# Six of the eight weight tiles of a first column block, split in advance into high and low halves

## The chip, the cores and the metric

The kernel runs on one core of one Trainium2 chip. The metric is the device time of one launch in microseconds. Engines are named as in the profile: PE is TensorE (PEld its weight loads), DVE is VectorE, ACT is ScalarE, POOL is GpSimd and SP is SyncE, which here only issues DMAs. POOL issues DMAs too.

## The reference, cut to what matters

Two blocks run one after the other on a sequence of 512 tokens with 1024 features, all in float32.

```python
def first_block(x, ...):
    x = x + 0.5 * swiglu(rmsnorm(x, ffn1_norm), ...)      # first gated layer
    ... two attentions ...
    x = x + 0.5 * swiglu(rmsnorm(x, ffn2_norm), ...)      # second gated layer: 1024 -> 2816 -> 1024
    x = rmsnorm(x, final_norm)
    return x

def token_mix(h, w_in, ...):                              # the mixer of the second block
    p = h @ w_in                                          # 1024 -> 2848
    ... convolution, recurrent scan ...
    return jnp.concatenate([u, y], axis=-1) @ w_out

def channel_mix(h, w_up, ...):
    z = causal_dwconv(h @ w_up, ffn_dw_w, ffn_dw_b)
    ...
```

`swiglu` is `(silu(h @ w_gate) * (h @ w_up)) @ w_down`. The change concerns the first 768 columns of the mixer's `w_in`: what is multiplied by them stays as it is.

## The kernel before, in words

**The three-part product.** Activations lie with features on the 128 partitions and tokens along the free axis. Every float32 operand is split into two parts, a rounded high half and the rest as a low half, and a product is three matmuls: high by high, high weight by low activation, low weight by high activation (`mm3`, L386). So every weight tile needs a split. `split_weights` (L375) does it at the time of use: SP issues the read into a `raw` tile, ACT copies it into the high half (L378), and DVE subtracts to get the low half (L379). There are two `raw` buffers, so a read waits until DVE is done with the read before the last one.

**Halves made in advance.** Some weights are split earlier and kept in DRAM. `make_halves` (L353) gives a list of pieces. A piece reads half the columns of one K tile (128 rows) into the one buffer `pre0` (POOL's queue, L363), DVE rounds it into `pre1` (the CAST of L365) and subtracts into `pre2` (L366), and POOL issues two writes to DRAM (L368). Each of the three buffers exists once. So the read of the next piece can start only after the subtraction of this one, and on POOL's queue it stands behind this one's two writes. Before the change the list has 32 pieces: 16 of 512 columns (`w_out2`, shown in some rows as `w_out`) and 16 of 384 columns (`up2k`). `halves_at` (L347) later loads both halves as they are, with two reads on SP's queue.

**Where the pieces run.** `swiglu` (L567) of the second gated layer takes two lists of side work, the modulation's (18 entries) and the pieces. Its first loop makes 22 pairs of gate and up column blocks and takes one entry of each list per pair. Its second loop, the down phase, makes output column blocks 0 to 6 (K = 2816, so 22 K tiles in weight chunks of 8, 8 and 6), and spreads over them what is left of the lists:

```python
n = -(-len(side) // (last - m))
weave(self.dense_steps(lambda: ps, down[m], hs, split=4), [(1.3, f) for f in side[:n]])
```

Block 7 follows in two halves of 256 tokens (`dense_halves`, L448). In the down phase only two weight slots exist, so the split of a chunk starts when PE has left the chunk before the last. At the end of a block `done` (L616) adds the result to `x` (L619, L620), sums squares (L512) and has POOL write `x` to DRAM (L624).

**Order.** The tile framework puts the instructions of each engine into one fixed order when the program is built, by its own estimates; a piece's two DVE operations stand at places in DVE's order that were chosen then. At run time each engine takes its instructions in that order.

**The mixer's first column blocks.** `first` (L1053) multiplies K tile by K tile into six column blocks at once (`group_halves`, L465): for each K tile the six products for tokens 0 to 255, then a second round for tokens 256 to 511. The split weights of all eight K tiles are kept for the second round, the first two in the ordinary weight slots and the others in buffers `kb`, `ra` and `vt` that the mixer uses later for something else (`room`, L1039). Those buffers lie in memory that the gated layer used before. While it runs, `enter(1, k)` (L659) prepares the second half of the tokens.

Of the kernel before, what the change touches and what calls it, by code (L numbers as in the profile page):

```python
# [11 lines left out]
F32 = mybir.dt.float32  # L12
# [7 lines left out]
P = 128  # L20
T = 512
D = 1024
KD = D // P
# [15 lines left out]
W_IN2 = [n for p in PH for n in p.split() if n[0] != "t" and n != "d1"]  # L39
# [216 lines left out]
class Net:  # L256
# [96 lines left out]
    def make_halves(self):  # L353


        nc, A = self.nc, self.A
        parts = ("w_out2", D), ("up2k", 768)
        self.made = {n: self.pd.tile([2, KD, P, w], F32, tag=n, name=n) for n, w in parts}

        def piece(name, k, c):  # L360
            n = c.stop - c.start
            raw, hi, lo = (self.pt.tile([P, T], dt, tag=f"pre{j}", name=f"pre{self._n()}") for j, dt in enumerate((F32, F32R, F32R)))
            nc.gpsimd.dma_start(raw[:, :n], A[name][k][:, c])  # L363
            with self.tc.issue_after(self.anchor):
                nc.vector.tensor_copy(hi[:, :n], raw[:, :n])  # L365
                nc.vector.tensor_sub(lo[:, :n], raw[:, :n], hi[:, :n].bitcast(F32))  # L366
            for half, t in enumerate((hi, lo)):
                nc.gpsimd.dma_start(self.made[name][half, k][:, c], t[:, :n].bitcast(F32))  # L368

        return [  # L370
            lambda name=name, k=k, c=c: piece(name, k, c)
            for name, w in parts for k in range(KD) for c in (slice(0, w // 2), slice(w // 2, w))
        ]

    def split_weights(self, raw, hi, lo, src, n):  # L375
# [608 lines left out]
    def mixer(self, acc1, acc2, stop):  # L984
        nc, A = self.nc, self.A
        nfg, dY, xs = self.nfg, self.dY, self.xin
# [15 lines left out]
        with self.phase("mix", False) as pa:  # L1002
# [49 lines left out]

            def first():  # L1053
                side = {2 + n: [lambda k=k: self.enter(1, k)] for n, k in enumerate((None, *range(KD)))}
                self.group_halves(lambda k, *a: self.weights_at(A["w_in2k"][k], *a), 6, xs, room, side, done=lambda m, ps: done(W_IN2[m])(ps), W=2)

            def residual():

# [4 lines left out]
            def shifted(j, out):  # L1063


                def f(ps):
                    n = ps.shape[0]
                    mu = self.v("mu", j)[:n]
                    nc.scalar.activation(out, ps, AF.Copy, scale=mu1[:n, j : j + 1])
                    nc.vector.scalar_tensor_tensor(  # L1070
                        out[:, 1:], ps[:, : T - 1], mu, out[:, 1:], op0=ALU.mult, op1=ALU.add
                    )

                return f
# [7 lines left out]
            def done(name):  # L1082
                if name == "w":
                    return shifted(0, wa)
                return {"k": k_done, "r": r_done, "v": v_done, "u": u_done, "g": ug_done, "d": gd_done}[name[0]](int(name[1]))
# [178 lines left out]
            def gate(f):  # L1264
# [5 lines left out]
                if f == 3:  # L1270
                    gt.extend((xt_(6), xt_(7), keep([P, T], "gd0"), keep([P, T], "gd1")))
                    for n, t in enumerate(gt):
                        nc.scalar.copy(t, st["gate", n])

            first()
            residual()
            ra = [keep([P, 2, T], f"ra{f}") for f in range(4)]
# [422 lines left out]
```

## Time and profile before

| What | us |
|---|---|
| median of 3 runs (lowest to highest) | 1691.19 (1685.33 to 1691.64) |
| profiled execution | 1682.04 |
| its span | 1680.3 |
| PE busy | 1647.0 (98%) |
| DVE busy | 1035.1 (62%) |
| ACT busy | 704.7 (42%) |
| POOL busy | 106.3 (6%) |

The profiled execution is one run; its span is what the views of the trace divide up, from 0 to 1680.3 us, and 1.7 us lie around it. Times in the rows are counted from the start of the span. A row of the timeline has the start and the length in us, the engine, the line, the operation, the output and the inputs, how many instructions were merged, and in brackets how long the engine stood idle before it and what ended that idle time.

### The profile page before, as it was taken

Reading aid. Unit: us, or ns where it says so; the run is one execution under the profiler, and the core shown is the slowest. Engines: PE = TensorE matmul, PEld = TensorE weight load, DVE = VectorE, ACT = ScalarE, POOL = GpSimd, SP = SyncE. Lnnn points to the kernel's source line nnn. Section 1 sums busy time; section 2 is a strip of 40 time slices with the busy share of each in tenths; the row PEclk is TensorE's granted clock in tenths of the full one; section 3 lists DMA queues with packets and bytes.
Section 4 is the critical chain, followed back from the end, with each engine's and each line's share of the span. In section 5 each row is a group of like instructions: output and inputs, shape, how many; then the busy total and the mean of one; then the engine's idle time right before and its main releaser. Section 6 shows DMA issues by size and latency. Waiting matters only on the chain.

```text
span 1680.3 us, 22030 instructions
## 1 busy us (share of the span) xinstructions
PE 1647.0 (98%) x8596; PEld 1334.7 (79%) x8596; DVE 1035.1 (62%) x1754; ACT 704.7 (42%) x1151; POOL 106.3 (6%) x200
## 2 busy tenths in 40 slices
PE   9999999999999999999999999999989999999997
PEld 6888888876776788888888887786869988888886
DVE  4554545546889565666445468998856675665224
ACT  5432232237669552232223254733346454444222
POOL 0000000000000002221122110000010000000000
PEclk9999999999999999999999999997989999999998
DMA  5344445534121226665455442232244023323332
GB/s 205 117 147 144 139 128 194 175 101 135 51 63 33 74 90 223 216 211 198 150 178 182 140 124 69 76 93 88 70 154 168 27 88 101 99 90 97 100 95 85
DMA packets 73081, 206.54 MB, mean 123 GB/s; under 512 B 18857, under 2 KB 21161, under 8 KB 72976
## 3 DMA queue, kind: packets, MB, share of 16 engines
q1 hardware_dynamic: 54320, 146.30, 26.9%
q0 software_dynamic: 16784, 56.73, 10.2%
q10 hardware_dynamic: 1872, 2.10, 0.4%
q8 instruction: 67, 1.10, 0.3%
q14 instruction: 38, 0.31, 0.1%
HBM read 183.87 MB, written 21.23 MB: 122 GB/s over the span
## 4 chain that ended last, share of the span: by engine, by line
PE 88%; DVE 6%; issue 2%; ACT 2%; DMA 2%; POOL 0%; ACTq 0%; DVEq 0%; POOLq 0%
PE ps L321 86%; PE ps L899 1%; DMA raw<-in_ffn_k 1%; DVE acc L512 1%; DVE Ts L1196 1%; DVE Tm L1193 0%; DVE wlo L379 0%; DMA Ts<-dY 0%; DMA raw<-in_w_in2k 0%; DVE x L1551 0%; DVE f L1645 0%; PE ps L1356 0%; DVE x L1646 0%; DVE x L1552 0%; ACT sq L511 0%
## 5 line engine op out<-in xcount | busy, mean ns | idle before, releaser
L378 ACT CAST whi<-raw 128x1024 fp32r<-128x1024 f32 (+1 forms) x240 | 245.3, 1022 | 625.7 <-PE ps L321 584.1
L379 DVE TENSOR_TENSOR wlo<-raw,whi 128x1024 fp32r<-128x1024 f32 (+1 forms) x240 | 284.5, 1186 | 238.0 <-ACT whi L378 232.9
L321 PE MATMUL ps<-xh,whi 128*128 128x512 f32 (+1 forms) x1008 | 400.0, 398 | 1.1 <-ACT xh L542 1.0
L321 PE MATMUL ps<-xh,wlo 128*128 128x512 f32 (+1 forms) x1008 | 390.9, 389 | 1.7 <-DVE wlo L379 1.6
L321 PE MATMUL ps<-xl,whi 128*128 128x512 f32 (+1 forms) x1008 | 391.0, 388 | 0.8 <-DVE xl L543 0.8
L321 PEld LDWEIGHTS ps<-xh,whi 128*128 128x128 f32 x1008 | 189.2, 188 | 51.5 <-issue 5.8
L321 PEld LDWEIGHTS ps<-xl,whi 128*128 128x128 f32 x1008 | 189.3, 188 | 44.5 <-issue 5.3
L321 PEld LDWEIGHTS ps<-xh,wlo 128*128 128x128 f32 x1008 | 188.9, 188 | 42.6 <-DVE wlo L379 2.8
L321 PE MATMUL ps<-hh,whi 128*128 128x512 f32 (+1 forms) x560 | 210.5, 376 | 0.0
L321 PE MATMUL ps<-hh,wlo 128*128 128x512 f32 (+1 forms) x560 | 209.8, 375 | 0.0
L321 PE MATMUL ps<-hl,whi 128*128 128x512 f32 (+1 forms) x560 | 209.8, 375 | 0.0
L321 PE MATMUL ps<-oh,whi 128*128 128x512 f32 (+1 forms) x360 | 134.5, 374 | 0.0
L321 PE MATMUL ps<-ol,whi 128*128 128x512 f32 (+1 forms) x360 | 134.1, 372 | 0.0
L321 PE MATMUL ps<-oh,wlo 128*128 128x512 f32 (+1 forms) x360 | 134.0, 372 | 0.0
L321 PEld LDWEIGHTS ps<-hh,whi 128*128 128x128 f32 x560 | 105.4, 188 | 19.7 <-issue 0.8
L321 PEld LDWEIGHTS ps<-hl,whi 128*128 128x128 f32 x560 | 105.4, 188 | 18.9
L321 PEld LDWEIGHTS ps<-hh,wlo 128*128 128x128 f32 x560 | 105.4, 188 | 18.9
L583 DVE TENSOR_TENSOR s<-s,ps 128x512 f32<-128x512 f32 x44 | 30.1, 687 | 133.0 <-PE ps L321 133.0
L321 PEld LDWEIGHTS ps<-oh,whi 128*128 128x128 f32 x360 | 67.7, 188 | 12.2 <-PE ps L321 0.2
L321 PEld LDWEIGHTS ps<-ol,whi 128*128 128x128 f32 x360 | 67.8, 188 | 12.1 <-issue 0.2
L321 PEld LDWEIGHTS ps<-oh,wlo 128*128 128x128 f32 x360 | 67.8, 188 | 11.8
L581 DVE TENSOR_TENSOR s<-ps,r 128x512 f32<-128x512 f32 x44 | 30.2, 691 | 56.0 <-PE ps L321 55.9
(446 smaller groups left out, 2237.2 us busy)
## 6 DMA issues: line engine op xcount, KB each, us to landing
raw<-in_ffn_gu SPq DMA_DIRECT2D x82, 512.0 KB, 4.2
ada<-in_ada_w POOLq DMA_DIRECT2D x48, 512.0 KB, 4.3
raw<-in_up SPq DMA_DIRECT2D x38, 512.0 KB, 3.5
raw<-in_ffn_d SPq DMA_DIRECT2D x32, 512.0 KB, 3.9
raw<-in_w_in SPq DMA_DIRECT2D x27, 512.0 KB, 3.5
w_out<-pre POOLq DMA_DIRECT2D x32, 256.0 KB, 4.6
raw<-in_down SPq DMA_DIRECT2D x16, 512.0 KB, 3.5
raw<-in_ffn_d SPq DMA_DIRECT2D x16, 384.0 KB, 3.1
```

What stands on the lines that cost most here:

```text
L321: self.nc.tensor.matmul(*a, **k)
L378: nc.scalar.copy(hi[:, :n], raw[:, :n])
L379: nc.vector.tensor_sub(lo[:, :n], raw[:, :n], hi[:, :n].bitcast(F32))
L512: nc.vector.tensor_add(acc, acc, s)
L581: nc.vector.tensor_mul(s, pg, r)
L583: self.anchor = nc.vector.tensor_mul(s, s, pu).ins
L899: nc.tensor.transpose(ps[:, i * P : (i + 1) * P], es[u, i][:, j * P : (j + 1) * P], self.c("ident"))
L1196: ins = nc.vector.tensor_add(t[:, i + 1 :, :c], t[:, i + 1 :, :c], o)
```

## The change

`make_halves` gets a third list of pieces, put ahead of the other two: K tiles 2 to 7 of the mixer's first 768 columns, 12 pieces of 384 columns. `first` then loads those six K tiles with `halves_at`, two reads each; K tiles 0 and 1 are split at the time of use as before.

```diff
@@ make_halves
-        parts = ("w_out2", D), ("up2k", 768)
-        self.made = {n: self.pd.tile([2, KD, P, w], F32, tag=n, name=n) for n, w in parts}
+        parts = ("w_in2k", 768, range(2, KD)), ("w_out2", D, range(KD)), ("up2k", 768, range(KD))
+        self.made = {n: self.pd.tile([2, KD, P, w], F32, tag=n, name=n) for n, w, _ in parts}
...
-            for name, w in parts for k in range(KD) for c in (slice(0, w // 2), slice(w // 2, w))
+            for name, w, ks in parts for k in ks for c in (slice(0, w // 2), slice(w // 2, w))
@@ mixer, first
-                self.group_halves(lambda k, *a: self.weights_at(A["w_in2k"][k], *a), 6, xs, room, side, done=lambda m, ps: done(W_IN2[m])(ps), W=2)
+                load = lambda k, *a: self.weights_at(A["w_in2k"][k], *a) if k < 2 else self.halves_at("w_in2k", k, *a)
+                self.group_halves(load, 6, xs, room, side, done=lambda m, ps: done(W_IN2[m])(ps), W=2)
```

The list of pieces grows from 32 to 44. The gate and up loop still takes 22 of them, so 22 are left for the down phase where there were 10.

DVE's order around one block of the down phase, block 5, before. `s` and `x` are the end of block 4, `wlo` the low halves of the weight chunks, `pre` the pieces, `acc` the sums of squares.

```order
L619 TENSOR_TENSOR s_7264<-ps_7171,r_4880 128x512
L620 TENSOR_TENSOR x_75<-x_75,s_7264 128x512
L379 TENSOR_TENSOR wlo_7307<-raw_7305,whi_7306 128x1024
L512 TENSOR_TENSOR acc_4875<-acc_4875,sq_7267 128x512
L365 CAST pre_7324<-pre_7323 128x384
L366 TENSOR_TENSOR pre_7325<-pre_7323,pre_7324 128x384
L512 TENSOR_TENSOR acc_4872<-acc_4872,sq_7270 128x512
L379 TENSOR_TENSOR wlo_7345<-raw_7343,whi_7344 128x768
L379 TENSOR_TENSOR wlo_7380<-raw_7378,whi_7379 128x1024
L619 TENSOR_TENSOR s_7367<-ps_7274,r_4880 128x512
```

And the same place of the changed kernel.

```order
L620 TENSOR_TENSOR x_75<-x_75,s_7329 128x512
L379 TENSOR_TENSOR wlo_7380<-raw_7378,whi_7379 128x1024
L512 TENSOR_TENSOR acc_4876<-acc_4876,sq_7332 128x512
L365 CAST pre_7316<-pre_7315 128x384
L366 TENSOR_TENSOR pre_7317<-pre_7315,pre_7316 128x384
L512 TENSOR_TENSOR acc_4872<-acc_4872,sq_7335 128x512
L379 TENSOR_TENSOR wlo_7418<-raw_7416,whi_7417 128x768
L365 CAST pre_7359<-pre_7358 128x384
L366 TENSOR_TENSOR pre_7360<-pre_7358,pre_7359 128x384
L365 CAST pre_7397<-pre_7396 128x384
L366 TENSOR_TENSOR pre_7398<-pre_7396,pre_7397 128x384
L379 TENSOR_TENSOR wlo_7461<-raw_7459,whi_7460 128x1024
```

One piece has become three, and two of them stand back to back ahead of the low half of the next chunk.

SP's queue at the start of the mixer, before: the reads for K tiles 1 to 5 of `first`, each into one of the two `raw` buffers.

```order
L377 DMA raw_7761<-in_w_in2k 128x768
L377 DMA raw_7785<-in_w_in2k 128x768
L377 DMA raw_7818<-in_w_in2k 128x768
L377 DMA raw_7845<-in_w_in2k 128x768
L377 DMA raw_7872<-in_w_in2k 128x768
```

And now, from K tile 1 on; `in_w_in` are the weights of the column blocks that follow `first`, `w_in2k` without the `in` the halves kept in DRAM.

```order
L377 DMA raw_7858<-in_w_in2k 128x768
L377 DMA raw_8218<-in_w_in 128x1024
L377 DMA raw_8260<-in_w_in 128x1024
L350 DMA kb_1101_7880<-w_in2k 128x768
L350 DMA kb_1102_7881<-w_in2k 128x768
L350 DMA kb_1105_7911<-w_in2k 128x768
L350 DMA kb_1106_7912<-w_in2k 128x768
L350 DMA ra_1107_7936<-w_in2k 128x768
L350 DMA ra_1108_7937<-w_in2k 128x768
L350 DMA ra_1109_7961<-w_in2k 128x768
L350 DMA ra_1110_7962<-w_in2k 128x768
L350 DMA vt_7986<-w_in2k 128x768 x4
```

Six reads became twelve, and two reads for later blocks now stand ahead of all twelve; each of the two needs a `raw` buffer, so the second waits until DVE has split K tile 1.

## Rows read from the trace of the kernel before

**Rows 1.** The page: busy time, share of the span and count by engine

```profile
PE 1647.0 (98%) x8596; PEld 1334.7 (79%) x8596; DVE 1035.1 (62%) x1754; ACT 704.7 (42%) x1151; POOL 106.3 (6%) x200
```

**Rows 2.** Busy time by stretch: length, engines, granted clock, DMA share, GB/s

```profile
862.00:963.00 101.00, 101.00 (x447) 83.65 (x446) 45.08 (x62) 27.61 (x32) 19.89 (x37) 1.00 0.54 173
984.00:1004.50 20.50, 16.81 (x121) 14.95 (x122) 14.76 (x29) 11.29 (x21) 3.56 (x11) 1.00 0.54 161
```

**Rows 3.** Timeline of DVE in the down phase, pieces and what stands between

```profile
865.59 0.36 DVE L365 CAST pre<-pre 128x384 fp32r<-128x384 f32 x1
...
871.01 0.36 DVE L365 CAST pre<-pre 128x384 fp32r<-128x384 f32 x1 [4.47 <-DMA pre<-in_up2k]
871.40 0.56 DVE L366 TENSOR_TENSOR pre<-pre,pre 128x384 fp32r<-128x384 f32 x1
...
876.62 0.36 DVE L365 CAST pre<-pre 128x384 fp32r<-128x384 f32 x1 [1.73 <-DMA pre<-in_up2k]
876.90 1.22 DVE L379 TENSOR_TENSOR wlo<-raw,whi 128x1024 fp32r<-128x1024 f32 x1
...
884.82 0.36 DVE L365 CAST pre<-pre 128x384 fp32r<-128x384 f32 x1 [4.26 <-DMA pre<-in_up2k]
...
890.45 0.40 DVE L365 CAST pre<-pre 128x384 fp32r<-128x384 f32 x1 [0.60 <-DMA pre<-in_up2k]
...
897.15 0.36 DVE L365 CAST pre<-pre 128x384 fp32r<-128x384 f32 x1 [1.68 <-DMA pre<-in_up2k]
```

**Rows 4.** Timeline of POOL in the same stretch: the issues of the pieces' reads

```profile
867.36 0.54 POOL L363 DMA_DIRECT2D pre<-in_up2k  x1
...
872.78 0.54 POOL L363 DMA_DIRECT2D pre<-in_up2k  x1
...
879.41 0.54 POOL L363 DMA_DIRECT2D pre<-in_up2k  x1
...
886.60 0.54 POOL L363 DMA_DIRECT2D pre<-in_up2k  x1
...
893.87 0.54 POOL L363 DMA_DIRECT2D pre<-in_up2k  x1
```

**Rows 5.** The tile `in_up2k`: the reads of the 384-column pieces

```profile
L363 POOL DMA_DIRECT2D pre<-in_up2k x16: 541/541/543, 797.1 to 938.2; - x16
...
DMA to landing us min/median/max: 2.8/3.2/5.3
```

**Rows 6.** Timeline of DVE at the ends of blocks 5 and 6

```profile
948.27 0.69 DVE L619 TENSOR_TENSOR s<-ps,r 128x512 f32<-128x512 f32 x1 [2.00 <-PE ps L321]
...
963.23 0.69 DVE L619 TENSOR_TENSOR s<-ps,r 128x512 f32<-128x512 f32 x1 [2.00 <-PE ps L321]
...
964.57 1.22 DVE L379 TENSOR_TENSOR wlo<-raw,whi 128x1024 fp32r<-128x1024 f32 x1
```

**Rows 7.** DMA issues: the 512-column pieces' reads, KB each, median us to landing

```profile
pre<-in_w_out POOLq DMA_DIRECT2D x16, 256.0 KB, 5.0
```

**Rows 8.** Timeline of PE in the mixer's first round: its waits, and K tile 7

```profile
986.80 0.38 PE L321 MATMUL ps<-xh,kb 128*128 128x256 f32 x1 [0.53 <-ACT kb L378]
...
991.25 0.38 PE L321 MATMUL ps<-xh,kb 128*128 128x256 f32 x1 [1.21 <-ACT kb L378]
...
992.25 0.50 PE L321 MATMUL ps<-xh,kb 128*128 128x256 f32 x2 [0.49 <-DVE kb L379]
...
1001.93 0.68 PE L321 MATMUL ps<-xh,vt 128*128 128x256 f32 x1
```

**Rows 9.** Timeline of SP: the issue of the read for K tile 3

```profile
985.30 0.33 SPq L377 DMA_DIRECT2D raw<-in_w_in2k  x1
```

**Rows 10.** Busy time by stretch, while the halves of `up2k` are loaded

```profile
1287.00:1289.00 2.00, 2.00 (x19) 2.00 (x18) 2.00 (x7) 0.84 (x2) 0.00 (x0) 1.00 0.82 318
```

**Rows 11.** Timeline of PE after a wait in the scan

```profile
1228.91 0.38 PE L321 MATMUL ps<-oh,kb 128*128 128x256 f32 x1 [1.76 <-ACT oh L383]
```

**Rows 12.** Busy time by stretch, some us behind that wait

```profile
1232.00:1234.00 2.00, 2.00 (x12) 2.00 (x10) 0.00 (x0) 0.00 (x0) 0.00 (x0) 0.50 0.00 0
```

## The prediction

> **What bounds the kernel now.** I read the page's busy times first: PE 1647.0 of 1680.3 us, DVE 62% [rows 1]. So the time is PE's work plus PE's waits, and an edit on another engine counts only where PE comes to wait for it, or ceases to. Next I cut the span at the two places that the change touches [rows 2]. In the down phase, 862 to 963, PE is busy for all 101 us at the full clock (2.4 GHz); nothing can be gained there, only lost. In the mixer's first round, 984 to 1004.5, PE is busy for 16.81 of 20.50 us; 3.7 us is the most that any edit there can give back.
>
> Then I read DVE and POOL in the down phase, since the list of pieces grows there from 10 to 22. The reader is to see in rows 3 that DVE already stands still for pieces: five CASTs begin after a wait for the piece's own read, 0.60 to 4.47 us, 12.7 us together. PE did not feel it only because few pieces come in a row: the low half of the next weight chunk was still in time.
>
> **The loop behind a piece.** One buffer holds the read, so pieces go round a ring, and the length of a turn follows from rows 3 and 4.
> - From the issue of a read to its CAST, where DVE stood waiting: 867.36 to 871.01 is 3.65, then 3.84, 5.41, 3.85 and 3.28 us. Over all sixteen of these reads the landing took 2.8 us at least and 3.2 in the middle [rows 5]; a CAST that waits starts some 0.3 us behind it.
> - From a CAST to the issue of the next read: 865.59 to 867.36 is 1.77, again 1.77 at 871.01, and 1.78 at 884.82. With a `wlo` between CAST and subtraction it is 2.79 (876.62 to 879.41), with other work there up to 3.42 (890.45 to 893.87).
>
> A turn takes 3.65 + 1.77 = 5.4 us at the usual speed. A block of the down phase takes PE 963.23 − 948.27 = 14.96 us [rows 6]. With one piece per block, as in blocks 3 to 6 before, the ring has time. With three per block it wants 16.3 us, and DVE's order is fixed: the CAST stands ahead of a `wlo`, so the `wlo` waits with it, and PE waits for the `wlo`.
>
> **The change part by part.**
> *Twelve pieces more.* 24 DVE operations of 0.36 and 0.56 us [rows 3] are 11 us of a DVE that is 45% busy in the down phase [rows 2]; as busy time they cost nothing, since PE's work covers them. 36 POOL issues of 0.54 us [rows 4] cost nothing as such either. In the gate and up loop the count per pair stays at one, and the new pieces are narrower than the 512-column ones that they displace there: nothing.
>
> *The ring in the down phase.* This is the term that decides. The changed order of DVE has 22 CASTs from the end of the gate loop to the last sum of block 6, thus 21 turns behind the first, which I leave at 865.6. Sixteen turns have nothing between CAST and subtraction or only what does not count, two have a `wlo` there, three an `x` or `acc`, which I put at 2.4 (1.77 and about 0.6): 16 × 1.77 + 2 × 2.79 + 3 × 2.4 = 41.1 us. Of the reads, sixteen are 192 KB; for these I take 3.65, the waited read that is nearest to 3.2 + 0.3. Five are 256 KB (`w_out2` now falls into the down phase); their landing took 5.0 in the gate loop, beside other traffic [rows 7]. I take 4.4, between both. 16 × 3.65 + 5 × 4.4 = 80.4. The last CAST then stands at 865.6 + 41.1 + 80.4 = 987.1. Behind it come its subtraction (0.9 for both), `s`, `x` and the `wlo` of block 7's second chunk, 963.23 to 965.79 before, 2.56 us [rows 6]: 990.5. Before, the same `wlo` was done at 965.8; block 7 uses up a chunk in half the time, so PE needs it about then. The loss is 24.7 us.
>
> Bounds of this term: all 21 reads at the shortest wait seen, 3.28, give 865.6 + 41.1 + 68.9 + 3.4 = 979.0, a loss of 13. Reads of 4.0 (the mean of the five) and 5.7 for the 256 KB ones give 1002.6, a loss of 37.
>
> *The mixer's first round.* Removed: six CASTs of ACT and six subtractions of DVE, behind which PE waited 0.53, 1.21 and 0.49 us [rows 8]. At best these 2.2 us go. Added: 12 reads of 384 KB (4.7 MB) where 6 were, behind a 512 KB read that cannot start before DVE has split K tile 1, at 985.30 in the old times, when the read into that buffer went out [rows 9]. All that is 5.2 MB. At 318 GB/s, the rate at which the like reads of `up2k` run later [rows 10], it takes 16.5 us. A 192 KB read needs 0.6 us at that rate and landed after 3.2 [rows 5], so 2.6 us come on top, and the last pair lands at 1004.4. PE wanted it at 1001.93 [rows 8]. So the wait for ACT turns into a wait for DMA, and PE comes out 2 us later. Ends: −2 if the reads all run ahead, +4 if POOL's small constants in the same stretch slow them. I take +2. Afterwards PE has the second round as before.
>
> *The sum.* On the profiled execution 1682.0 + 24.7 + 2 = 1708.7 us. The median of the runs shown is 9.2 above that execution; 1691.2 + 26.7 gives a forecast of 1718 us, slower by 1.6%.
>
> **A page of the skill beside it.** The waited reads took 3.28 to 5.41 us from issue to use [rows 3, 4]. The Trainium skill, page "DMA: Bandwidth & Descriptors", section "Anatomy of one DMA — SWDGE (gpsimd) path", fits a DMA from POOL's queue at about 2.0 us plus its bytes over 436 kB per us. An estimate by it for 192 KB is 2.45 us, under the 2.8 us of the fastest read here [rows 5], so the trace disagrees; by it the ring would turn in 4.2 us, three turns would fit into a block, and the down phase would lose nothing, which is the first rival below.
>
> **The rivals.**
> *1. Not slower: the reads come fast enough.* The loss is gone if 865.6 + 41.1 + 21 × L + 3.4 stays at 965.8, so at L = 2.65 us or less. For it: the traffic from SP slows down whenever PE waits, so a read may find a freer way. Against it: none of the sixteen landed under 2.8 [rows 5], which makes some 3.1 to the CAST. Then only the mixer's −2 to +4 counts: 1689 to 1695, no change that can be told. It decides below 2.65 and loses 21 us for each us above.
>
> *2. The clock falls as well.* PE would wait in stretches of 1 to 6 us. In the scan PE waited 1.76 us and was granted 0.50, the 1.2 GHz level, some 3 us later [rows 11, 12]. If each of about ten stalls were followed by 3 us at half the clock, that would be up to 15 us more: 1733. Against it: in the mixer's first round PE waited for 3.7 of 20.5 us and kept 1.00 [rows 2], and a slower PE in a stretch that DVE's waits set costs only in part.
>
> *3. The change works as a saving.* The pieces hide and the mixer gives its 2.2 us: 1689. It is under what can be told, and the lot of reads behind 985.30 speaks against it [rows 9, 10].
>
> **How the numbers follow.** The ring binds, clock kept: 0.78. Rival 1: 0.07. Rival 2: 0.13. Rival 3: 0.02. The range of the likeliest case goes from the lowest run with its low bound, 1685 + 13 = 1698, to the highest run with the high one and the mixer's 2, 1692 + 37 + 2 = 1731. With parts of rival 2 inside, about 8 in 10 lie in 1698 to 1731. What a measurement of this kernel can tell from no change is about 0.5%, 8.5 us. Slower than that: the ring but for its lowest tail, and rival 2: 0.88. Within: rivals 1 and 3 and that tail: 0.10. Faster: 0.02, since all of PE's idle time in the mixer's first round is 3.7 us.
>
> **What the new profile would show.** Right: PE idle in the down phase, put down to `wlo` of L379, about 25 us in all; CASTs of L365 that wait for `pre<-in_w_out` or `pre<-in_up2k` some twenty times; blocks of 16 to 20 us instead of 14.96, the longer where two pieces stand ahead of a `wlo`; in the mixer's first round PE waiting for reads into `kb`, `ra` and `vt` instead of ACT. Wrong: blocks still 14.96 us apart, which would mean that the reads take under 2.7 us; or a loss without waits of DVE for reads, which would take the ring out of it; or a granted clock well under 1.00 in the down phase, which is rival 2.

## The result, and the profile after

| | before | after |
|---|---|---|
| median of 5 runs, us | 1687.73 (1683.71 to 1691.64) | 1725.64 (1720.72 to 1731.64) |
| profiled execution, us | 1682.04 | 1730.54 |
| its span, us | 1680.3 | 1728.8 |

The changed kernel is slower by a factor of 1.0247, 95% interval 1.022 to 1.0274: some 38 us by the medians.

The busy times of the page barely answer to that [rows 1]: PE has 23 us more with the same 8596 products, which points to a lower granted clock in places (below), and DVE, with 24 operations added and six taken away, 4 us more.

```profile
PE 1669.9 (97%) x8596; PEld 1350.8 (78%) x8596; DVE 1039.2 (60%) x1772; ACT 700.3 (41%) x1145; POOL 125.1 (7%) x236
```

The same stretch of the down phase as in [rows 2], and then the whole stretch up to the last piece (length, engines, granted clock, DMA share, GB/s):

```profile
862.00:963.00 101.00, 89.63 (x366) 70.96 (x365) 43.66 (x66) 21.76 (x26) 29.67 (x55) 0.95 0.61 198
862.00:1000.00 138.00, 116.13 (x480) 92.76 (x479) 59.87 (x92) 30.55 (x37) 39.91 (x74) 0.93 0.59 192
```

PE now stands still for 21.9 of 138 us, and DVE is less busy than before in the first 101 us, though it was given more to do: it waits. The granted clock is 0.93 over these 138 us, where it was 1.00 before. The waits of 862 to 1000 say for what (total us, times, longest):

```profile
DVE pre L365 <- DMA pre<-in_up2k: 52.0, 16, 4.5
...
PE ps L321 <- DVE wlo L379: 21.9, 11, 5.0
DVE pre L365 <- DMA pre<-in_w_out: 20.8, 6, 5.7
```

All 22 CASTs wait for their own reads, 72.8 us together. Two places of DVE's timeline show how that reaches PE. In the first, the end of block 0 and the whole of block 1; in the second, the end of block 6:

```profile
874.70 0.69 DVE L619 TENSOR_TENSOR s<-ps,r 128x512 f32<-128x512 f32 x1
...
880.03 0.43 DVE L365 CAST pre<-pre 128x512 fp32r<-128x512 f32 x1 [2.79 <-DMA pre<-in_w_out]
...
887.79 0.43 DVE L365 CAST pre<-pre 128x512 fp32r<-128x512 f32 x1 [5.74 <-DMA pre<-in_w_out]
888.26 0.69 DVE L366 TENSOR_TENSOR pre<-pre,pre 128x512 fp32r<-128x512 f32 x1
888.87 1.22 DVE L379 TENSOR_TENSOR wlo<-raw,whi 128x1024 fp32r<-128x1024 f32 x1
894.58 0.43 DVE L365 CAST pre<-pre 128x512 fp32r<-128x512 f32 x1 [4.50 <-DMA pre<-in_w_out]
895.04 0.69 DVE L366 TENSOR_TENSOR pre<-pre,pre 128x512 fp32r<-128x512 f32 x1
895.65 0.68 DVE L619 TENSOR_TENSOR s<-ps,r 128x512 f32<-128x512 f32 x1
...
995.00 0.36 DVE L365 CAST pre<-pre 128x384 fp32r<-128x384 f32 x1 [3.99 <-DMA pre<-in_up2k]
995.87 0.68 DVE L619 TENSOR_TENSOR s<-ps,r 128x512 f32<-128x512 f32 x1
997.20 1.22 DVE L379 TENSOR_TENSOR wlo<-raw,whi 128x1024 fp32r<-128x1024 f32 x1
```

Block 1 takes 895.65 − 874.70 = 20.95 us instead of 14.96 [rows 6]. The `wlo` at 888.87 stands directly behind a piece in DVE's order, and it cannot begin before the piece's read has come. Even the `s` of a finished block waits for a CAST. The last line answers to 964.57 in [rows 6]: 32.6 us later. At the end of block 7 the loss is 33.9, behind the mixer's first round 35.9. The span is 48.5 us longer; nearly all of the other 12.6 us are lost in the scan, the recurrent part of the mixer, which takes 193.5 us instead of 180.0, and the experiments show that they are no part of the change.

### The profile page after: what moved, and what is told of

Its sections match the earlier page's. It is cut to its first block, busy times and chain, and to the rows that moved or that the text cites. A ratio compares the mean times of both kernels' runs of the same rounds, so it can differ in the third digit from the quotient of the medians.

```text
span 1728.8 us, 22142 instructions
## 1 busy us (share of the span) xinstructions
PE 1669.9 (97%) x8596; PEld 1350.8 (78%) x8596; DVE 1039.2 (60%) x1772; ACT 700.3 (41%) x1145; POOL 125.1 (7%) x236
## 3 DMA queue, kind: packets, MB, share of 16 engines
q1 hardware_dynamic: 55184, 148.66, 26.7%
## 4 chain that ended last, share of the span: by engine, by line
PE 80%; DVE 7%; issue 6%; DMA 3%; POOL 2%; ACT 2%; SPq 0%; POOLq 0%; DVEq 0%; ACTq 0%
PE ps L321 78%; PE ps L899 1%; POOL up2k L368 1%; DMA pre<-in_up2k 1%; DMA raw<-in_ffn_k 1%; DMA kb<-w_in2k 1%; DVE wlo L379 1%; DVE acc L512 1%; POOL pre L363 0%; DVE Ts L1197 0%; DVE Tm L1194 0%; DMA pre<-in_w_out 0%; POOL w_out L368 0%; DMA Ts<-dY 0%; PE ps L1357 0%
## 5 line engine op out<-in xcount | busy, mean ns | idle before, releaser
L321 PE MATMUL ps<-hh,wlo 128*128 128x512 f32 (+1 forms) x560 | 214.8, 384 | 21.9 <-DVE wlo L379 21.9
L321 PEld LDWEIGHTS ps<-xl,whi 128*128 128x128 f32 x1008 | 189.3, 188 | 44.7 <-issue 5.3
L321 PEld LDWEIGHTS ps<-xh,wlo 128*128 128x128 f32 x1008 | 188.9, 188 | 42.4 <-DVE wlo L379 2.8
L321 PE MATMUL ps<-hh,whi 128*128 128x512 f32 (+1 forms) x560 | 214.0, 382 | 0.0
L321 PE MATMUL ps<-hl,whi 128*128 128x512 f32 (+1 forms) x560 | 213.3, 381 | 0.0
```

Of the source, the lines that this page charges most:

```text
L321: self.nc.tensor.matmul(*a, **k)
```

## The experiments

Losses below are from the traces, each against the same instruction of the first trace of before: to the end of block 7 (its second `s`, 983.96 before), and from there to the first tap of the convolution behind the mixer's first round (1013.28 before). Ratios are against before, with the 95% interval, of five runs or more.

| run | ratio | to the end of block 7 | mixer's first round |
|---|---|---|---|
| the changed kernel | 1.0247 (1.022 to 1.0274) | +33.9 | +2.0 |
| made, not used | 1.0204 (1.018 to 1.0229) | +34.4 | −0.6 |
| loads only | 1.0006 (0.9988 to 1.0025) | +0.2 | +1.7 |
| read one piece ahead | 1.0085 (1.0061 to 1.0109) | +6.9 | +3.4 |
| two per pair | 1.0220 (1.0193 to 1.0246) | +28.8 | +1.9 |
| deep buffers | 1.0034 (1.0014 to 1.0054) | +1.4 | +1.9 |
| six pieces more | 1.0055 (1.0034 to 1.0076) | +7.5 | +0.7 |
| four pieces more | 1.0024 (1.0007 to 1.0041) | +0.2 | +1.4 |
| small pieces | 1.0098 (1.0075 to 1.0121) | +16.9 | −0.1 |
| all pieces on POOL | 1.0406 (1.0378 to 1.0434) | +60.2 | +2.0 |
| last 22 on POOL | 1.0238 (1.0213 to 1.0264) | +40.3 | +1.6 |

The kernel before, executed once more, stands at +0.5 and −0.6 us in the last two columns, so half a us there tells nothing.

**Made, not used.** The changed kernel, but `first` splits its weights as before.

```diff
-                load = lambda k, *a: self.weights_at(A["w_in2k"][k], *a) if k < 2 else self.halves_at("w_in2k", k, *a)
+                load = lambda k, *a: self.weights_at(A["w_in2k"][k], *a)
```

> All 44 pieces are made as in the changed kernel, but first() loads and splits its weights as the kernel before does; the twelve extra pieces are not used. Theory (ring of the pieces in the down phase): the down phase loses what it loses in the changed kernel, 33.9 us in the profile up to the end of block 7, and the mixer's first round is back at the old 20.5 us; 2 us less than the changed kernel, ratio to before about 1.021 to 1.024. Rival (the loads of first() are what costs): 1.000 to 1.005. Open: the 12 us that the changed kernel's profile loses in the scan; if they belong to the pieces they are here again, if they are a matter of one execution they may be anything.

1720.32 us against 1686.52, a ratio just under the expected one: the whole loss of the down phase is there with none of the loads. The scan took 4.6 us more than before in this profile.

**Loads only.** The list of 32 pieces; K tiles 2 to 7 come from halves that exist anyway, those of `up2k`.

```diff
-        parts = ("w_in2k", 768, range(2, KD)), ("w_out2", D, range(KD)), ("up2k", 768, range(KD))
+        parts = ("w_out2", D, range(KD)), ("up2k", 768, range(KD))
...
-... else self.halves_at("w_in2k", k, *a)
+... else self.halves_at("up2k", k, *a)
```

> The list of pieces is the old one of 32; first() loads K tiles 2 to 7 from the halves of up2k, which have the same shape (so its numbers are not the reference's). Theory: the down phase is as before, blocks of 14.96 us; the mixer's first round costs 2 us more than before, PE waiting for reads into kb and ra instead of ACT; ratio 1.001, at most 1.002. Rival (the mixer's loads carry a good part of the 38 us): 1.005 to 1.02. Rival (they save, -2 us): 0.999. If the 12 us in the scan come from how first() gets its weights, they show here.

1687.21 us, no difference that can be told. These two runs split the change into its halves: the making costs, the using costs 1.7 us. The loads run the DMAs nearly full, as the window behind the first reads shows:

```profile
994.00:999.00 5.00, 4.17 (x34) 4.17 (x35) 5.00 (x13) 2.72 (x7) 0.00 (x0) 1.00 1.02 371
```

**Read one piece ahead.** Of each piece the read is issued one piece earlier, into a second `pre0`.

```diff
+        def read(name, k, c):
+            raw = self.pt.tile([P, T], F32, tag="pre0", name=f"pre{self._n()}", bufs=2)
+            nc.gpsimd.dma_start(raw[:, : c.stop - c.start], A[name][k][:, c])
+            return raw
...
-            nc.gpsimd.dma_start(raw[:, :n], A[name][k][:, c])
+            raw = ready.pop(0) if ready else read(name, k, c)
+            if todo:
+                ready.append(read(*todo.pop(0)))
```

> Pieces as in the changed kernel, same number, place and work, but the read of each piece is issued one piece earlier into a second buffer, so a turn of the ring no longer holds read and subtraction one behind the other. Theory (the loss is the wait of DVE for the piece's own read): no CAST waits, blocks of 14.96 us again, granted clock 1.00 in the down phase; only the mixer's 2 us stay, ratio 1.000 to 1.004. Rival (DVE's 24 more operations, or the traffic of the extra reads and writes): nothing changes, 1.02 to 1.025. Rival (half: reads grow longer than a turn because two run at a time): 1.008 to 1.015.

1.0085 is not the theory's number; it lies in the range of the second rival, but not for that rival's reason. The waits of DVE in the down phase say why:

```profile
DVE pre L372 <- DMA up2k<-pre: 14.4, 9, 2.6
DVE pre L373 <- DMA up2k<-pre: 11.8, 5, 4.5
DVE pre L373 <- DMA w_out<-pre: 7.7, 5, 2.2
DVE pre L372 <- DMA w_out<-pre: 7.6, 6, 2.4
```

No CAST waits for a read any more. CAST and subtraction now wait until the piece before has been written out of the one `pre1` and the one `pre2`: the ring had a second link behind the first. PE's waits are down to 4.2 us.

**Deep buffers.** That link cut too: two buffers for `pre1`, and the low half written over the read, which has three.

```diff
+            hi = self.pt.tile([P, T], F32R, tag="pre1", name=f"pre{self._n()}", bufs=2)
+            lo = raw.bitcast(F32R)
```

> As the run with the reads one piece ahead, and the second link cut as well: there 27 waits of DVE (16.. 12 us and more for the CASTs alone) were for the writes of the piece before to leave the one pre1 and the one pre2. Here pre1 has two buffers and the low half is written over the read, which has three. Same pieces, same places, same bytes. Theory (DVE waits for the pieces' buffers, reads first, then writes): the 8.4 us that the down phase still lost go as well, only the mixer's 1.9 us stay, ratio 1.000 to 1.003. Rival (what was left are DVE's 24 operations or the traffic): 1.006 to 1.009 as before.

1.0034; the down phase loses 1.4 us. Its first 101 us:

```profile
862.00:963.00 101.00, 100.68 (x442) 82.41 (x441) 55.71 (x85) 27.36 (x32) 37.59 (x69) 1.00 0.75 250
```

More traffic (250 GB/s against 198 after and 173 in [rows 2]) and a busier DVE (55.7 us against 43.7 and 45.1), with PE busy for 100.7 of 101 us. So the bytes and DVE's operations cost at most the 1.4 us that are left; the buffers cost the rest.

**Two per pair.** The extra pieces taken by the gate and up loop, the down phase left with ten.

```diff
+                if new2 is not None and m < 12:
+                    side[1].pop(0)()
```

> The twelve extra pieces are taken by the gate and up loop, two per pair in the first twelve pairs, one in the others; the down phase has its old 10 pieces. Theory: a pair takes PE over 30 us, two turns of 5 to 7 us fit; the down phase is as before; only the mixer's 2 us stay, ratio 1.000 to 1.004. Rival (a piece costs wherever it stands, by DVE's or POOL's time): 1.01 to 1.025.

A miss of mine: 1.0220. I had the length of a pair wrong; it is 10.9 us, as the trace of before shows (709.91 to 720.79):

```profile
709.91 0.69 DVE L581 TENSOR_TENSOR s<-ps,r 128x512 f32<-128x512 f32 x1 [0.68 <-PE ps L321]
...
720.79 0.69 DVE L581 TENSOR_TENSOR s<-ps,r 128x512 f32<-128x512 f32 x1 [1.22 <-PE ps L321]
```

The 24 CASTs of those pairs are 6.8 us apart (630.12 to 786.18), two are 13.6 us, and 12 pairs would lose 32 us by that; 28.8 was lost. From 570 to 862 CASTs waited 69.4 us for their reads and PE 20.5 us for `wlo`; in the trace of before neither wait is there. The down phase lost nothing. The ring holds; the figure that I had put beside it did not.

**Six and four pieces more.** Only K tiles 5 to 7, and only K tiles 2 and 3; the others are split in `first` as before.

```diff
-        parts = ("w_in2k", 768, range(2, KD)), ...
+        parts = ("w_in2k", 768, range(5, KD)), ...
-... if k < 2 else self.halves_at(...)
+... if k < 5 else self.halves_at(...)
```

```diff
-        parts = ("w_in2k", 768, range(2, KD)), ...
+        parts = ("w_in2k", 768, range(2, 4)), ...
-... if k < 2 else self.halves_at(...)
+... if k not in (2, 3) else self.halves_at(...)
```

> Six pieces more instead of twelve (K tiles 5 to 7), one buffer each as in the changed kernel: 16 pieces of 384 columns in the down phase, 3 in blocks 0 and 1, 2 in the others. Theory (ring): a turn is 6.0 us by the changed kernel's trace (3.93 for the read, some 2.0 from CAST to read); three want 18 us of 14.96, two 12. So blocks 0 and 1 lose about 3 us each and the others nothing: 4 to 8 us in the down phase, 0 to 2 in the mixer, ratio 1.003 to 1.006. Rival (each piece costs its share of the 33.9 us, 2.8 us, by DVE's time or traffic): 17 us, 1.010.

> Four pieces more (K tiles 2 and 3 alone, those behind whose split PE waited 0.53, 1.21 and 0.49 us before): 14 pieces of 384 columns in the down phase, two per block. Theory: 12 us of turns in 14.96 us of block, no loss in the down phase or up to 2 us where two stand back to back ahead of a wlo; the mixer loads 2 MB less than in the changed kernel, so its waits for DMA stay out and up to 2 us come back; ratio 0.998 to 1.002. Rival (2.8 us for each piece): 11 us, 1.006.

Both as the ring has it: four pieces more cost the down phase 0.2 us, six 7.5, twelve 33.9. The single blocks I had less well: with six more, nearly all falls on block 1. Measured by DVE's `s`, which itself stands behind a CAST there, block 1 takes 24.70 us (873.70 to 898.40) and block 2 12.52, together 7.3 more than twice 14.96. The gain hoped for with four did not come either; the mixer's first round is 1.4 us longer, not shorter.

**Small pieces.** The extra twelve last, 48 columns wide, unused; `first` as in "made, not used".

```diff
-        parts = ("w_in2k", 768, range(2, KD)), ("w_out2", D, range(KD)), ("up2k", 768, range(KD))
+        parts = ("w_out2", D, range(KD)), ("up2k", 768, range(KD)), ("w_in2k", 96, range(2, KD))
```

> 44 pieces, but the twelve extra ones stand last, are 48 columns wide (24 KB) and unused; first() splits its weights as before. In the down phase blocks 0 to 2 have ten 384-column pieces (4, 3, 3), blocks 3 to 6 three small ones each. Theory: blocks 0 to 2 lose 3 to 9 us each where 24 or 18 us of turns stand against 14.96, 12 to 15 us in all; a small piece's turn is the fixed part of a read and of its issue and CAST, 4 to 4.6 us by the fastest reads seen, so blocks 3 to 6 are 14.96 us long again. Ratio 1.006 to 1.010. Rival (the time of a turn doesn't depend on bytes): blocks 3 to 6 lose 3 us each, 1.014 to 1.017. Rival (not the ring but traffic): blocks 3 to 6 lose nothing, and blocks 0 to 2, with their usual traffic and three or four pieces, lose in proportion to bytes.

The reads of 24 KB, by their tile:

```profile
L363 POOL DMA_DIRECT2D pre<-in_w_in2k x12: 539/539/542, 921.2 to 975.8; - x12
...
DMA to landing us min/median/max: 1.9/3.0/5.0
```

An eighth of the bytes, and in the middle 3.0 us where the ten reads of 192 KB ahead of them in the down phase took 3.7: most of a read's length at these sizes does not go with its bytes. (The traffic beside them was not the same.) The small CASTs are 4.8 us apart (925.00 to 977.86, eleven turns) against 5.9 for the ten wide turns ahead of them (859.47 to 918.85). Three turns of 4.8 fit into a block: blocks 4 to 6 take 12.18, 16.04 and 14.98 us, together less than three times 14.96. The loss, 16.9 us against the 12 to 15 expected, lies in blocks 1 to 3; the wide pieces reached into block 3, and the first small turn in it was longer than a wide one (925.00 to 931.61). The bytes of a piece shorten its turn, so the first rival is out; what traffic costs by itself is settled by the deep buffers.

**All pieces on POOL.** To take the wait off DVE, the two operations of a piece go to POOL.

```diff
-                nc.vector.tensor_copy(hi[:, :n], raw[:, :n])
-                nc.vector.tensor_sub(lo[:, :n], raw[:, :n], hi[:, :n].bitcast(F32))
+                nc.gpsimd.tensor_copy(hi[:, :n], raw[:, :n])
+                nc.gpsimd.tensor_sub(lo[:, :n], raw[:, :n], hi[:, :n].bitcast(F32))
```

> As the changed kernel, one buffer each, same pieces; only the two operations of a piece run on POOL instead of DVE. A turn of the ring is no shorter than before (rather longer), but the engine that waits for the read is no longer the one whose low halves PE needs. Theory (what costs is that a waiting CAST holds back the wlo behind it in DVE's order): no wait of PE for wlo in the down phase, blocks of 14.96 us, only the mixer's 2 us stay: ratio 1.000 to 1.004. Rival (the extra reads and writes, or operations of POOL beside DVE's, slow DVE's own low halves): 1.006 to 1.03, without waits of DVE for reads.

1.0406, the worst of all and far from the theory's 1.000 to 1.004. The last CAST began at 883 already, in the gate and up loop, and the loss is there; the blocks of 14.96 us behind it show nothing, as no piece is left in them. POOL, then DVE, then PE around one stall:

```profile
764.66 0.54 POOL L363 DMA_DIRECT2D pre<-in_w_out  x1
765.20 0.54 POOL L949 DMA_DIRECT2D ada<-in_ada_w  x1
769.50 0.61 POOL L365 CAST pre<-pre 128x512 fp32r<-128x512 f32 x1 [3.76 <-DMA pre<-in_w_out]
```

```profile
772.68 1.41 DVE L959 SCALAR_TENSOR_TENSOR adas<-ada,silu_c,adas 128x512 f32<-128x512 f32 x2 [5.47 <-DMA ada<-in_ada_w]
774.01 0.69 DVE L384 TENSOR_TENSOR hl<-s,hh 128x512 fp32r<-128x512 f32 x1
774.62 1.22 DVE L379 TENSOR_TENSOR wlo<-raw,whi 128x1024 fp32r<-128x1024 f32 x1
```

```profile
775.89 0.79 PE L321 MATMUL ps<-xh,wlo 128*128 128x512 f32 x1 [3.58 <-DVE wlo L379]
```

The modulation's reads (`ada`) stand on POOL's queue, now behind pieces that wait. DVE waits for `ada`, the `wlo` behind it waits too, and PE for the `wlo`. From 570 to 915 DVE waits 58.9 us for `ada` (not at all before) and PE 39.2 us for `wlo`. The wait had been moved to another queue, and that queue had a customer on the path as well.

**The last 22 on POOL.** So only the down phase's pieces, where no `ada` is left.

```diff
+                self.np = getattr(self, "np", 0) + 1
+                e = nc.vector if self.np <= 22 else nc.gpsimd
+                e.tensor_copy(hi[:, :n], raw[:, :n])
+                e.tensor_sub(lo[:, :n], raw[:, :n], hi[:, :n].bitcast(F32))
```

> The first 22 pieces, those of the gate and up loop, are made by DVE as in the changed kernel; only the last 22, those of the down phase, are made by POOL, where the modulation's reads no longer stand in the queue. One buffer each; by the run with all pieces on POOL a turn takes 6.6 to 7.2 us there, so 22 of them want about 150 us from 860 on and are done near 1010, some 25 us behind the end of the down phase. Theory (a waiting CAST costs because of what is queued behind it on its engine): no wait of PE for wlo in the down phase, blocks of 14.96 us, the end of block 7 at 984 as before; then 2 us in the mixer, and up to 10 us if one of the small reads that the mixer has on POOL's queue behind the pieces comes too late: ratio 1.001 to 1.007. Rival (extra traffic, or POOL's operations beside DVE's, cost by themselves): PE waits for wlo in the down phase again, 1.01 to 1.025.

The down phase is untouched, with the traffic of the changed kernel: PE is busy for all of its window, and the ends of blocks 5 and 6 are 14.96 us apart again. DVE's own low halves of 1024 columns do take longer beside POOL's operations, 1.33 us on average over this window instead of 1.22, but PE does not come to wait for them. The lines are that window, then DVE at these ends and at three waits behind them, then PE:

```profile
862.00:963.00 101.00, 101.00 (x447) 83.62 (x446) 39.53 (x43) 27.63 (x32) 50.68 (x71) 1.00 0.63 196
```

```profile
948.59 0.69 DVE L621 TENSOR_TENSOR s<-ps,r 128x512 f32<-128x512 f32 x1 [2.00 <-PE ps L321]
...
963.55 0.69 DVE L621 TENSOR_TENSOR s<-ps,r 128x512 f32<-128x512 f32 x1 [1.30 <-PE ps L321]
...
995.03 1.26 DVE L676 SCALAR_TENSOR_TENSOR x<-x,col,acc 128x256 f32<-128x256 f32 x1 [12.64 <-DMA dY<-x]
1012.33 0.48 DVE L676 SCALAR_TENSOR_TENSOR x<-x,col,acc 128x256 f32<-128x256 f32 x1 [16.04 <-DMA dY<-x]
1022.70 0.48 DVE L676 SCALAR_TENSOR_TENSOR x<-x,col,acc 128x256 f32<-128x256 f32 x1 [9.88 <-DMA dY<-x]
```

```profile
1025.62 1.65 PE L321 MATMUL ps<-xh,wlo 128*128 128x256 f32 x6 [41.04 <-DVE wlo L381]
```

That settles the mechanism: a slow ring costs nothing where the engine that waits has nothing urgent behind it. The time is 1.0238 all the same, which I had not foreseen: the writes of `x` to DRAM (`dY`) stand on POOL's queue among the pieces, `enter` may overwrite `x` only when they are done, and PE waits once for 41.0 us. That wait begins at 984.6, when PE is through with block 7; the +40.3 of the table is DVE's `s`, which stands behind the waits for `dY`.

**Both kernels again.**

> The changed kernel once more, for its profile. Theory: the down phase loses 33 to 35 us and the mixer's first round 2 again, and the scan is another length than the 193.5 us (first di of L1379 to first zv of L1615) of the first profile, between 179 and 194 as in the eight experiments; 1720 to 1732 us. Rival (the scan's 13.5 us belong to the change): 193 us again.

> The kernel before once more, for its profile. Theory: the same trace up to the scan, to some tenths of a us, and a scan of another length than the 180.0 us of the first profile, 179 to 194; 1681 to 1694 us. Rival (the scan of the kernel before is always 180 us): 180 again.

1718.75 and 1681.24 us, one execution each. The changed kernel lost 34.0 and 2.3 us again, and its scan took 181.2 us instead of 193.5. So the 13.5 us that the scan lost in the first profile are not the change's. For the kernel before my expectation was wrong: 180.5 after 180.0. The thirteen traces other than that first one of the changed kernel have 179.6 to 189.3 us for the same instructions.

No version beats the kernel before; the nearest are loads alone (no difference) and four pieces more (1.0024).

## Why the prediction was right, and where it was short

*Slower, by the ring in the down phase:* right. Making without using gives the loss, using without making does not, and cutting the ring's links takes all but 1.4 us of the loss away with the bytes and DVE's work unchanged.

*The size.* Forecast 26.7 us, range 7 to 40; 38 by the medians, 35.9 in the trace without the scan (36.3 in the second one). What remains between 35.9 and 38 I leave to the scan's spread; that is not shown. The term that was too small is the ring, 24.7 forecast and 32.6 measured at the same `wlo`. The last CAST came at 995.00 and not at 987.1; the 7.9 us are these:
- The 16 reads of 192 KB took 3.93 us from issue to CAST on average, not 3.65, and the five of 256 KB 4.55, not 4.4: 5.2 us. I had taken the reads' median landing from a trace in which few pieces followed each other, 3.2 us; their median is now 3.9.

```profile
L363 POOL DMA_DIRECT2D pre<-in_up2k x16: 543/543/543, 902.7 to 990.7; - x16
...
DMA to landing us min/median/max: 2.8/3.9/4.9
```

- The first CAST came at 867.01, not at 865.6, behind a 256 KB read instead of a 192 KB one: 1.4 us.
- From CAST to the next read: 42.4 us in all, not 41.1. A 512-column subtraction takes 0.69 us and not 0.56, so those turns have 1.98 (867.01 to 868.99) and not 1.77.

```profile
868.99 0.54 POOL L363 DMA_DIRECT2D pre<-in_w_out  x1
```

The prediction also puts 0.3 us between a landing and the CAST that waits for it; its own rows show 0.1 (the read issued at 867.36 landed after 3.5 us, its CAST began after 3.65). The sum does not rest on that, as it takes 3.65 from a row, but rival 1 does: the fastest landing of 2.8 makes 2.9 to the CAST and not 3.1, still above 2.65.

My upper bound, 37 us, took reads of 4.0 and 5.7; the mean of the waited reads in [rows 3, 4] would have been the better forecast.

*The page of the skill beside it.* The small pieces measure the point: in their run the reads of 24 KB took 1.9 us at the fastest and 3.0 in the middle, all sixteen of 192 KB 2.8 and 3.4. The Trainium skill, page "DMA: Bandwidth & Descriptors", section "Anatomy of one DMA — SWDGE (gpsimd) path", gives 2.0 us plus bytes over 436 kB per us; an estimate by it is 2.06 and 2.45. The trace agrees with the 0.4 us between the two, in the middle of all of them (it is 0.7 against the ten of the down phase), and with the fastest read of 24 KB; the middle ones took about 1 us more than the estimate.

*The mixer's first round, +2:* the size is right (2.0, 1.7 and 2.3), the reason only in part. PE's waits there, after; the first is as long before (1.43 us at 985.30):

```profile
1019.15 0.98 PE L321 MATMUL ps<-xh,wlo 128*128 128x256 f32 x6 [1.43 <-DVE wlo L379]
1021.59 3.20 PE L321 MATMUL ps<-acc,cst 128*128 128x256 f32 x6 [1.46 <-DVE acc L512]
...
1028.58 0.36 PE L321 MATMUL ps<-xh,kb 128*128 128x256 f32 x1 [1.24 <-ACT xh L675]
...
1030.90 0.97 PE L321 MATMUL ps<-xh,kb 128*128 128x256 f32 x6 [0.92 <-DMA kb<-w_in2k]
```

The last two are for reads, as forecast, but at K tile 3 and not at the last pair. The trace puts the one at 1028.58 down to `xh` of `enter`, but the read of K tile 3's high half, issued at 1020.5, landed after 7.9 us, at the same time. In the second profile of the changed kernel both are put down to reads:

```profile
1028.42 0.35 PE L321 MATMUL ps<-xh,kb 128*128 128x256 f32 x1 [0.98 <-DMA kb<-w_in2k]
...
1031.32 0.97 PE L321 MATMUL ps<-xh,kb 128*128 128x256 f32 x6 [1.50 <-DMA kb<-w_in2k]
```

The wait for `acc` I had not seen. Before, the products for the sums stand behind the 18 of K tile 2 (`kb`), without a wait:

```profile
989.01 1.03 PE L321 MATMUL ps<-acc,cst 128*128 128x256 f32 x4
```

Now they stand ahead of them, directly behind K tile 1 (1019.15 and 1021.59 above), where the sums are not ready. In "four pieces more" the product for the sums waits 1.86 us. The waits for ACT's split [rows 8] went, as said; these took their place.

The three new waits are 3.6 us where the three of [rows 8] were 2.2, so they make 1.4 of the 2.0 us. In the rest the clock has a part, which the prediction had left at 1.00 here: behind the first two waits PE was granted the 1.2 GHz level for a while. In "made, not used", where the loads are the old ones, the clock was 1.00 over the whole round.

```profile
1023.00:1025.00 2.00, 2.00 (x5) 0.92 (x4) 0.48 (x1) 1.48 (x4) 0.31 (x1) 0.50 1.02 404
```

*Rival 1 (the reads come fast enough):* wrong; its point was 2.65 us, and even 24 KB reads are above it in the middle (3.0).

*Rival 2 (the clock falls as well):* it did fall, and cost little. Behind its longest wait, 5.0 us, PE was granted the 1.2 GHz level:

```profile
967.00:972.00 5.00, 0.16 (x1) 0.00 (x0) 1.91 (x3) 0.57 (x1) 1.84 (x5) 0.90 0.40 133
972.00:977.00 5.00, 4.80 (x11) 3.80 (x12) 1.99 (x5) 0.25 (x1) 0.92 (x2) 0.50 0.54 182
```

But up to 995.00 every CAST waited for its read, so the chain of reads and CASTs set the time and a slower PE only waited less. Only behind it does the clock add: 997.20 to the end of block 7 takes 20.6 us where it took 19.4, with 0.50 granted from 998.4 to 1001.4, behind a wait of 4.3 us.

*Signs.* PE's idle time on `wlo` 21.9 us (about 25 expected), 22 waits of CASTs (some twenty); six of the blocks between 17.1 and 23.8 us (16 to 20 expected).

## What to carry to other kernels

Work that hides in another engine's idle time must be counted by the length of its loop (read, compute, next read), not by its busy time: one piece per block was free, two were free, three cost 34 us. In a fixed order a waiting instruction holds up all that stands behind it on its engine, so ask of each engine that could take the wait what is queued there and who needs it; moving it to another queue moved the stall to another customer, twice. What frees such a loop is buffers, on the read's side and on the write's. Whether the loss also goes when the pieces are put behind the `wlo` in DVE's order was not tried.

## What the runs showed of the hardware

Reads on POOL's queue of 24 KB and of 192 KB differed by 0.4 us in the middle (3.0 and 3.4 in one run) and by 0.9 at the fastest (1.9 and 2.8). DVE's subtractions of 128x1024 took 1.33 us on average while POOL made the pieces, and 1.22 before; one took 1.92. The scan of one and the same program took 193.5 us in one execution and 181.2 in another. With it went the granted clock, which stayed at 0.50, the 1.2 GHz level, for longer in the first. Three windows of the first profile of the changed kernel, and one of its second, where the scan begins within half a us of the same time:

```profile
1206.00:1216.00 10.00, 9.33 (x63) 8.26 (x61) 6.65 (x11) 0.58 (x1) 0.00 (x0) 0.50 0.04 7
1216.00:1226.00 10.00, 10.00 (x104) 9.41 (x103) 3.90 (x7) 2.91 (x5) 0.00 (x0) 0.50 0.09 15
1226.00:1236.00 10.00, 9.33 (x117) 8.59 (x117) 6.69 (x11) 1.43 (x3) 0.00 (x0) 0.78 0.05 8
```

```profile
1216.00:1226.00 10.00, 9.33 (x151) 8.62 (x148) 8.49 (x14) 3.66 (x7) 0.00 (x0) 1.00 0.09 15
```

What makes it stay there in one execution and not in another was not found out.
